# A hybrid decoder layer in one core: the second set's first product moved ahead in the first queries and keys, and one weight split moved between two additions of the output projection

## The chip, the cores and the metric

The kernel runs on one core of a Trainium2 chip. The metric is the device time of one execution in microseconds (us); lower is better. Runs of one kernel are summed up by their median.

## The reference

One decoder layer on x of 512 tokens by 1024 channels, all in float32, cut here to what the change touches:

```python
u = rmsnorm(x, ln1_g[i])
proj = u @ w_in[i]
q, k, v, pool_in, z, xbc, dt_raw, gate_pre = jnp.split(proj, split_idx, axis=-1)
y_a = dilated_attention_mixer(q, k, v, rel_bias) @ w_a[i]
y_b = pool_mixer(pool_in, pool_w[i], pool_scale[i]) @ w_b[i]
y_c = ssd_mixer(z, xbc, dt_raw, ...) @ w_c[i]
merged = gates[:, :, 0] * y_a + gates[:, :, 1] * y_b + gates[:, :, 2] * y_c
x = x + merged @ w_o[i]
x = x + conv_ffn(rmsnorm(x, ln2_g[i]), ...)
```

The attention has three groups of six heads of 64. The first group's queries and keys, 384 columns each, are three blocks of 128 columns of w_in for q and three for k. The output projection is `merged @ w_o`, 512x1024 by 1024x1024.

## The kernel before

**Jobs.** The work is a list of jobs, written by the generator `program`. A job is one piece of a weight matrix and the products that use it. Each float32 weight is split in two: a high part `wh`, rounded by a cast on ScalarE (`cast`, L200), and a low part `wl`, weight minus high part, by VectorE (`low`, L220). The activations are split in the same way. A product is then three groups of matmuls (`mm3`, L239), in the order wh by the high activation, wh by the low activation, wl by the high activation. So the low part of a weight is needed only for the last third of a product's matmuls. There are three buffers for high parts, two for low parts, and two for raw weights.

**Preparing ahead.** The loop at the end runs the jobs in order. Ahead of the body of job n it calls `prepare`, which issues the low part of job n+1, the cast of job n+2, and the load of job n+3. A job's `form` gives its weight where that isn't loaded but lies in a tile that sums are made in, and its `then` is run right behind its low part. A job that is marked `at_once` has the cast that it prepares issued whole at that place; otherwise the cast comes in two halves, between the matmuls of its body (`second`, `flush`). With `low_apart` the low part of the next job is not issued by `prepare` but kept as `low_next`, for the body to call. Each of TensorE, ScalarE, VectorE and GpSimd works off its instructions in the order in which the program issues them (`manual_schedule`); SyncE issues the loads.

**Sets of seven.** A product of two by two blocks is done in seven products in place of eight, "one" to "seven", with sums of weight quarters and of activations (`sevens`, `set_of_sevens`). `W[0]` and `W[1]` are quarters in memory. "one" uses W[0] as loaded; its `then`, `first_sum`, adds W[1] to W[0] on VectorE (L354) and issues two DMAs on GpSimd's queue that add another quarter into W[1] in memory (L375). "five" uses W[0] after that sum. "two" and "three" have raw quarters of their own, and "seven" uses W[1] after the two accumulating DMAs.

The queries and keys of the first group are two sets: set 0, with two blocks of q and two of k (256 columns a job, 24 matmuls of 128x256), and set 1, the half set, with the third block of each (128 columns, 12 matmuls). Both start from weights loaded far ahead: two loads (L750) and four (L745). Four banks of PSUM (`ROLE`) serve set 0 and set 1's "one", "six", "seven" and "four". They are taken from the rotation that the job before, the second of `v_jobs`, uses for its four accumulators `pb`; they come free when ScalarE has copied them out, each in two copies, v (L586) and dtr (L588). The first job of set 0 takes the first of them.

The second v job is `at_once`. `prepare` ahead of it issues the low part of set 0's "one" with the sum behind it, and the cast of the job after that; then come its matmuls, the copies of its banks, and a step of other work: one block of the pooling branch, as a difference pd on VectorE (L976), its cast pdh on ScalarE (L978), and its low part pdl on VectorE (L979). GpSimd makes the running sums psw for it (L967, L968). sal and sbl (L338, L339) are low parts of the activation sums that "five" and others use.

**Output projection.** `wo_sevens` does `merged @ w_o` in seven jobs in the order one, two, five, three, six, seven, four, each of 24 matmuls of 128x512 in two halves (i = 0, 1). After each half `use` adds the bank into the residual (L1369). "five" opens the banks Z; "three" goes on adding into the same banks. A bank that is being read by an addition can't be added to by a later product until the addition is done. `norm_early` (L446) starts the next norm on GpSimd.

Of the kernel before, what the change touches and what calls it, by code (L numbers as in the profile page):

```python
# [83 lines left out]
def trunk(ctx: ExitStack, tc, out, x, rel_bias, ln1_g, w_in, b_gate, w_a, pool_w, pool_scale, w_b,  # L84
# [23 lines left out]
    def T(name, dt=F32, shape=(P, S)):  # L108
        return big.tile(list(shape), dt, name=name, tag="t")
# [321 lines left out]
    def norm_turn(us, uh, ul, tb):  # L431
        for h in range(2):
            ps = SM("uT")
            for j in range(4):
                pe.transpose(ps[:, j * P:(j + 1) * P], us[h][:, j * P:(j + 1) * P], eye)
            pv = ps.rearrange("p (j t) -> p j t", j=4)
            hh = uh[:, 4 * h:4 * h + 4, tb * P:(tb + 1) * P]
            act.copy(hh, pv)  # L438
            dve.tensor_sub(ul[:, 4 * h:4 * h + 4, tb * P:(tb + 1) * P], pv, hh.bitcast(F32))

    def norm_early(t, g, h=0, mean=True):

        ss, v0 = (cpool.tile([P, 1], F32, name=f"{n}_{len(V0)}") for n in ("s0", "v0"))
        xg = T("xg")
        squares(act, t, ss)
        pool.tensor_tensor(xg, t, g[:, h * S:h * S + S], OP.mult)  # L446
        V0.append((v0, ss))
        if mean:
            mean_of(v0, ss)
        return v0, xg  # L450
# [4 lines left out]
    def norm_late(t, g, v0, outs, both=False, h=1):  # L455

        ss, v, sq, r, rt = (small(n, [P, 1]) for n in ("ss", "v", "sq", "r", "rt"))
        squares(act, t, ss)
        xg = T("xg")
        dve.tensor_tensor(xg, t, g[:, h * S:h * S + S], OP.mult)  # L460
        dve.scalar_tensor_tensor(v, ss, 1.0 / D, v0, OP.mult, OP.add)
        act.activation(sq, v, AF.Sqrt)
        yield xg
        dve.reciprocal(r, sq)
        dve.scalar_tensor_tensor(rt, r, v, r, OP.mult, OP.mult)
        dve.tensor_scalar(rt, rt, -0.5, 1.5, OP.mult, OP.add)
        if both:
            dve.tensor_tensor(r, r, rt, OP.mult)
            (o, a), (p, b) = outs(xg)
            dve.tensor_scalar(o, a, r, None, OP.mult)  # L470
            act.mul(p, b, r)
            return
        for o, src in outs(xg):
            dve.tensor_scalar(o, src, r, rt, OP.mult, OP.mult)
# [873 lines left out]
    def wo_sevens():  # L1348

        q = lambda two, h: w_o[:, h * S:h * S + S].rearrange("(k two p) c -> two p k c", two=2, p=P)[two]  # L1350
        W, X, Y, Z, r, means = {}, {}, {}, {}, {}, []

        def load():
            both_ = upool.tile([P, KD, S], F32R, name="ws", tag="uh").bitcast(F32)
            W["five"], W["six"] = both_[:, :4, :], both_[:, 4:, :]
            sp.dma_start(W["five"], q(0, 0))
            sp.dma_start(W["six"], q(1, 1))

        def add():
            for name, src in (("seven", q(0, 1)), ("four", q(1, 0))):  # L1360
                W[name] = ypool.tile([P, 4, S], F32, name="w3", tag="xs")
                sp.dma_start(W[name], src)
            for name, src in (("five", q(0, 1)), ("seven", q(1, 1)), ("six", W["five"]),
                              ("four", W["six"])):
                for k in (0, 2):
                    pool.dma_start(W[name][:, k:k + 2, :], src[:, k:k + 2, :], accum_op=OP.add)

        def plus(tb, h, what, op=OP.add):
            dve.tensor_tensor(X1[tb, h], X1[tb, h], what, op)  # L1369

        def late_norm(tb, h):
            if "uh" not in nxt:
                nxt["uh"] = upool.tile([P, KD, S], F32R, name="uh2", tag="uh")
                nxt["ul"] = upool.tile([P, KD, S], F32R, name="ul2", tag="ul")
            v0, xg0 = nxt[tb]
            us = [T("u0"), T("u1")]
            it = norm_late(X1[tb, h], nxt["g2"], v0, lambda xg1: ((us[1 - h], xg0), (us[h], xg1)),
                           True, h)
            next(it)

            def rest():
                next(it, None)
                yield
                norm_turn(us, nxt["uh"], nxt["ul"], tb)
            return rest()

        def use(name, i):
            if name == "one":
                plus(i, 0, X[i])
                if i:  # L1390
                    next(pair_sums[3])
                    next(pair_sums[3])
            elif name == "two":
                plus(i, 0, Y[i])
                nxt[i] = norm_early(X1[i, 0], nxt["g2"], mean=False)
                means.append(V0[-1])
            elif name == "five":
                plus(2 + i, 1, Z[i])
            elif name == "three":
                plus(i, 1, Z[i])  # L1400
                if i:
                    for _ in range(2):
                        mean_of(*means.pop(0))
            elif name == "six":
                plus(i, 1, X[i], OP.subtract)
                r[i] = late_norm(i, 1)
                if i:
                    next(r[0])
                    next(r[1])
            elif name == "seven":  # L1410
                plus(2 + i, 1, X[i], OP.subtract)
                nxt[2 + i] = norm_early(X1[2 + i, 1], nxt["g2"], 1, mean=False)
                means.append(V0[-1])
                if i:
                    next(r[0], None)
                    next(r[1], None)
                else:
                    jobs[name].low_next()
            else:
                if i:  # L1420
                    late_split.pop(0)()
                plus(2 + i, 0, X[i])
                mean_of(*means.pop(0))
                r[i] = late_norm(2 + i, 0)
                late.append(r[i])
                if i == 0:
                    next(r[i])

        banks = {"one": X, "six": X, "seven": X, "four": X, "five": Z, "three": Z, "two": Y}
        jobs = {}  # L1430

        def make(name, source=None):
            def body(ws):
                wh, wl = ws
                parts = [MS[SIDES[name], p] for p in range(4)]
                fresh = name in ("one", "two", "five")
                if name == "two":
                    for _ in pair_sums[3]:
                        pass
                if name == "four":  # L1440
                    late_split.append(jobs[name].prepare(later=True))
                if name == "one":
                    for i in range(2):
                        Y[i] = MM("p2")
                    for i in range(2):
                        X[i] = MM("p1")
                if name == "five":
                    for i in range(2):
                        Z[i] = SM("p5")
                for i in range(2):  # L1450
                    o = slice(i * P, (i + 1) * P)
                    mm3(banks[name][i], lambda k: wh[:, k, :], lambda k: wl[:, k, :],
                        lambda k: parts[k][0][:, o], lambda k: parts[k][1][:, o], range(4),
                        fresh, True, flip=True, again=not fresh)
                    use(name, i)
                    if i:
                        step()
            job = jobs[name] = Job([source] if source is not None else [], 4, S, body)
            if source is None:
                job.load = lambda: None  # L1460
                job.form = lambda: W[name]
            job.late = name == "four"
            job.at_once = True
            job.low_apart = name == "seven"
            return job

        return load, add, [make("one", q(0, 0)), make("two", q(1, 0)), make("five"),
                           make("three", q(1, 1)), make("six"), make("seven"), make("four")]


# [236 lines left out]
    def program():  # L1707
# [9 lines left out]
        for i, job in enumerate(v_jobs(0)):  # L1717
            job.at_once = True
            yield job
            if i == 0:  # L1720
                yield Call(lambda: ahead(sets0[0][1][n] for n in ("two", "three")))
        for i, name in ((0, "one"), (0, "five"), (1, "one"), (0, "two"), (1, "five"), (0, "three"),
                        (1, "two"), (1, "three"), (0, "six"), (1, "six"), (0, "seven"), (1, "seven"),
                        (0, "four"), (1, "four")):
            yield sets0[i][1][name]
# [77 lines left out]
    jobs = list(program())  # L1803
# [219 lines left out]
```

## Time and profile before

| | us |
|---|---|
| median of 3 runs | 1032.05 |
| lowest, highest run | 1031.59, 1032.14 |
| profiled execution, its time | 1030.83 |
| its span, first to last instruction | 1029.1 |
| TensorE busy | 1015.2 |
| VectorE busy | 738.8 |
| ScalarE busy | 502.7 |
| GpSimd busy | 181.3 |

The mean granted clock of TensorE is 0.996. Times inside the profile count from the span's start. Rows of the order of time give the start, the duration, the engine, the line of the kernel, the operation, output and inputs with their sizes, how many instructions are merged, and in brackets the idle time ahead of it on that engine and what ended it. PE is TensorE, DVE is VectorE, ACT is ScalarE, POOL is GpSimd, SP is SyncE, PEld is TensorE's load of the stationary operand. A matmul's duration reaches over the start of the next one, so merged rows overlap a little.

### The profile page before, as it was taken

How to read it: one execution, taken by the hardware profiler on the slowest of the kernel's cores; microseconds unless marked ns; L12 is line 12 of the kernel's file. 1: busy time of each engine (PE TensorE's matmuls, PEld its weight loads, DVE VectorE, ACT ScalarE, POOL GpSimd, SP SyncE). 2: the span in 40 equal slices, each digit the busy share in tenths (PEclk: the TensorE clock that was granted, in tenths of full speed). 3: DMA queues.
4: the chain of work that ended last, by engine and by line, in shares of the span. 5: the costliest groups of instructions: out<-in, count | busy, mean ns of one | idle time of the engine just before them, and what ended most of it. 6: DMA issues, size and time to landing. Idle time of an engine off the chain costs nothing.

```text
span 1029.1 us, 14051 instructions
## 1 busy us (share of the span) xinstructions
PE 1015.2 (99%) x5504; PEld 867.5 (84%) x5504; DVE 738.8 (72%) x1022; ACT 502.7 (49%) x859; POOL 181.3 (18%) x147
## 2 busy tenths in 40 slices
PE   9998999999999999999999999999999999999997
PEld 9988878899998888888888888898888888888885
DVE  6786775777767758767668768866768677666775
ACT  6434655445536664566455235654444443443342
POOL 1592000001100004310144611201111001111120
PEclk9998999999999999999999999999999999999999
DMA  9326521137543335552243779333233224323142
GB/s 295 107 67 127 190 83 45 62 63 193 130 111 123 89 98 148 135 135 59 82 150 128 268 145 285 123 122 105 82 118 118 91 82 164 123 83 122 61 144 82
DMA packets 122129, 127.11 MB, mean 124 GB/s; under 512 B 5811, under 2 KB 103414, under 8 KB 122063
## 3 DMA queue, kind: packets, MB, share of 16 engines
q1 hardware_dynamic: 115999, 118.02, 36.4%
q0 software_dynamic: 5472, 7.34, 4.7%
q8 instruction: 43, 0.70, 0.3%
q10 hardware_dynamic: 592, 0.86, 0.2%
q14 instruction: 23, 0.19, 0.1%
HBM read 120.31 MB, written 2.22 MB: 119 GB/s over the span
## 4 chain that ended last, share of the span: by engine, by line
PE 92%; POOL 3%; DVE 2%; issue 1%; ACT 1%; DMA 0%; SPq 0%; POOLq 0%; DVEq 0%; ACTq 0%
PE pa L239 30%; PE p L239 22%; PE pu L239 22%; PE pqk L239 3%; PE pb L239 2%; PE pa L1870 2%; POOL psw L967 2%; PE ps L850 1%; PE pu L1638 1%; PE pt L878 1%; PE ppw L239 1%; PE po L891 1%; PE py L1176 1%; POOL psw L968 1%; PE pa L1827 1%
## 5 line engine op out<-in xcount | busy, mean ns | idle before, releaser
L220 DVE TENSOR_TENSOR wl<-raw,wh 128x2048 fp32r<-128x2048 f32 (+3 forms) x88 | 192.6, 2190 | 36.2 <-ACT wh L200 23.3
L200 ACT CAST wh<-raw 128x1024 fp32r<-128x1024 f32 (+3 forms) x174 | 166.9, 980 | 47.7 <-DVE raw L344 25.5
L1499 DVE SCALAR_TENSOR_TENSOR hc<-pu,fcol,hc 128x510 f32<-128x510 f32 x88 | 65.9, 748 | 59.9 <-ACT hc L1496 58.2
L239 PE MATMUL pa<-uh,wh 128*128 128x512 f32 x336 | 86.5, 399 | 0.0
L239 PE MATMUL pu<-uh,wl 128*128 128x512 f32 (+1 forms) x352 | 83.7, 380 | 0.0
L239 PE MATMUL pu<-uh,wh 128*128 128x512 f32 (+1 forms) x352 | 83.6, 380 | 0.0
L239 PE MATMUL pu<-ul,wh 128*128 128x512 f32 (+1 forms) x352 | 83.5, 379 | 0.0
L239 PE MATMUL pa<-ul,wh 128*128 128x512 f32 x336 | 83.0, 389 | 0.0
L239 PE MATMUL pa<-uh,wl 128*128 128x512 f32 x336 | 83.0, 389 | 0.0
L1504 POOL TENSOR_TENSOR hc<-hc 128x512 f32<-128x512 f32 x22 | 30.4, 1380 | 274.8 <-DVE hc L1499 225.9
L239 PEld LDWEIGHTS pu<-uh,wl 128*128 128x128 f32 x352 | 64.1, 188 | 12.8 <-DVE wl L220 0.3
L239 PEld LDWEIGHTS pu<-uh,wh 128*128 128x128 f32 x352 | 64.1, 188 | 12.6 <-ACT uh L438 0.2
L239 PEld LDWEIGHTS pu<-ul,wh 128*128 128x128 f32 x352 | 64.2, 188 | 12.5
L239 PEld LDWEIGHTS pa<-ul,wh 128*128 128x128 f32 x336 | 63.1, 188 | 13.3
L239 PEld LDWEIGHTS pa<-uh,wl 128*128 128x128 f32 x336 | 63.1, 188 | 13.1
L239 PEld LDWEIGHTS pa<-uh,wh 128*128 128x128 f32 x336 | 61.2, 188 | 12.8 <-issue 0.7
L1496 ACT ACTIVATE hc<-pu,fcol,fcol 128x512 f32<-128x512 f32 x40 | 31.2, 780 | 81.3 <-PE pu L239 81.0
L200 ACT CAST wh<-w 128x512 fp32r<-128x512 f32 (+3 forms) x78 | 50.1, 686 | 28.8 <-DVE w L354 17.2
L220 DVE TENSOR_TENSOR wl<-w,wh 128x1024 fp32r<-128x1024 f32 (+3 forms) x39 | 54.0, 1385 | 10.6 <-ACT wh L200 5.8
L375 POOL DMA_DIRECT2D w<-in_w_in_dram x14 | 17.2, 1231 | 194.1 <-DVE w L354 140.2
L871 ACT ACTIVATE sb<-sb,both 128x128 f32<-128x128 f32 (+1 forms) x72 | 30.1, 418 | 31.8 <-DVE both L868 21.7
L1501 ACT ACTIVATE hc<-hc 128x512 f32<-128x512 f32 x22 | 13.9, 632 | 42.9 <-DVE hc L1499 42.9
(400 smaller groups left out, 2033.9 us busy)
## 6 DMA issues: line engine op xcount, KB each, us to landing
raw<-in_ffn_w_up_dram SPq DMA_DIRECT2D x22, 1024.0 KB, 5.1
raw<-in_w_in_dram SPq DMA_DIRECT2D x21, 1024.0 KB, 5.3
raw<-in_ffn_w_down_dram SPq DMA_DIRECT2D x11, 1024.0 KB, 4.8
raw<-in_w_in_dram SPq DMA_DIRECT2D x16, 512.0 KB, 4.9
raw<-in_w_b_dram SPq DMA_DIRECT2D x4, 1024.0 KB, 4.7
al<-ad SPq DMA_DIRECT2D x16, 256.0 KB
raw<-in_w_c_dram SPq DMA_DIRECT2D x4, 1024.0 KB, 5.3
w<-in_ffn_w_down_dram SPq DMA_DIRECT2D x4, 1024.0 KB
```

Source lines behind the costliest of these rows:

```text
L200: act.copy(job.high[:, :, o], job.raw[:, :, o])
L220: (eng or dve).tensor_tensor(l[:, :, o], job.raw[:, :, o], h[:, :, o].bitcast(F32), OP.subtract)
L239: pe.matmul(ps, l, r, start=first and n == 0, stop=last and n == total - 1, skip_group_check=again)
L375: pool.dma_start(W[1][:, k:k + 2, at:at + n], src[:, k:k + 2, :], accum_op=OP.add)
L850: pe.matmul(pss[i][:, o:o + w * P], q[r, n * P:(n + 1) * P], k[r, kb * P:(kb + w) * P], start=True, stop=True)
L871: act.activation(sb[:, off:off + w * P], sb[:, off:off + w * P], AF.Exp, bias=nm[:, n, h:h + 1], accum_out=ls[:, n, h:h + 1])
L967: pool.tensor_tensor(nxt[:, sh:], cur[:, sh:], cur[:, :S - sh], OP.add)
L1496: act.activation(t, ps, AF.Identity, bias=ff["c1"][:, ff["b"] + m:ff["b"] + m + 1], scale=fw(2, m))
L1499: dve.scalar_tensor_tensor(t[:, sh:], ps[:, :S - sh], fw(k, m), t[:, sh:], OP.mult, OP.add)
L1501: act.activation(t, t, AF.Silu)
L1504: pool.tensor_tensor(a, a, t, OP.mult)
L1870: pe.matmul(first[2 * n + j][:, lo:hi], a[:, k, j * P:(j + 1) * P], b[:, k, lo:hi], start=a is wh and b is uh and k == 0, stop=a is wl and ...
```

## The change

Two edits that have no instruction in common. In the order of the first sets, set 1's "one" comes second, ahead of set 0's "five" and not behind it. In the output projection the third job, "five", is marked `low_apart`, and the low part of the fourth job, "three", is issued by `use` after the first of the two additions of "five", where it was issued ahead of the matmuls of "five". No instruction is added or taken away.

```diff
             elif name == "five":
                 plus(2 + i, 1, Z[i])
+                if i == 0:
+                    jobs[name].low_next()
...
             job.at_once = True
-            job.low_apart = name == "seven"
+            job.low_apart = name in ("five", "seven")
...
-        for i, name in ((0, "one"), (0, "five"), (1, "one"), (0, "two"), (1, "five"), (0, "three"),
+        for i, name in ((0, "one"), (1, "one"), (0, "five"), (0, "two"), (1, "five"), (0, "three"),
                         (1, "two"), (1, "three"), (0, "six"), (1, "six"), (0, "seven"), (1, "seven"),
                         (0, "four"), (1, "four")):
             yield sets0[i][1][name]
```

## The prediction

> **What bounds the kernel now.** I read the page first (busy time of each engine), then the list of who waited for whom on TensorE, then the busy and clock table of four short stretches, then the order of time of every engine around the two places that the change touches.
>
> ```profile
> PE 1015.2 (99%) x5504; PEld 867.5 (84%) x5504; DVE 738.8 (72%) x1022; ACT 502.7 (49%) x859; POOL 181.3 (18%) x147
> ```
> ```profile
> PE p L239 <- ACT dtr L588: 4.7, 1, 4.7
> ```
> ```profile
> 77.80:81.20 3.40, 0.53 (x3) 1.00 0.85 246
> 81.20:84.60 3.40, 1.53 (x7) 0.50 1.00 221
> 84.60:88.00 3.40, 3.40 (x18) 0.50 0.45 73
> 88.00:91.40 3.40, 3.40 (x30) 0.99 0.63 77
> ```
>
> TensorE is the bound: it is busy 1015.2 us of a span of 1029.1, so only 13.9 us are idle, and one wait holds 4.7 of them. What does not shorten a wait of TensorE or raise its clock is worth nothing. In the table of stretches (start:end, length, PE busy, count, granted clock, DMA share, GB/s) the reader sees a second price of that wait: the clock falls to 0.50 after the stretch in which TensorE was busy 0.53 of 3.4 us, and stays there for 6.8 us.
>
> **Place one, the first sets of seven products.** All engines in order of time:
>
> ```profile
> 77.45 0.89 PE L239 MATMUL pb<-wl,uh 128*128 128x400 f32 x4
> 83.06 1.22 PE L239 MATMUL p<-uh,wh 128*128 128x256 f32 x4 [4.73 <-ACT dtr L588]
> 88.23 0.64 PE L239 MATMUL p<-sah,wh 128*128 128x256 f32 x4
> 91.10 0.64 PE L239 MATMUL p<-uh,wh 128*128 128x256 f32 x4
> 92.54 0.64 PE L239 MATMUL p<-uh,wh 128*128 128x256 f32 x4
> 73.42 0.62 ACT L978 CAST pdh<-pd 128x512 fp32r<-128x512 f32 x1 [3.39 <-DVE pd L976]
> 81.42 1.14 ACT L200 CAST wh<-w 128x512 fp32r<-128x512 f32 x2 [7.39 <-DVE w L354]
> 82.84 0.17 ACT L588 COPY dtr<-pb 128x16 f32<-128x16 f32 x1
> 84.73 0.78 ACT L200 CAST wh<-w 128x256 fp32r<-128x256 f32 x2
> 77.63 0.69 DVE L338 TENSOR_TENSOR sal<-sa,sah 128x512 fp32r<-128x512 f32 x1 [1.74 <-POOL psw L968]
> 78.87 1.21 DVE L220 TENSOR_TENSOR wl<-w,wh 128x1024 fp32r<-128x1024 f32 x1
> 80.11 1.22 DVE L354 TENSOR_TENSOR w<-w 128x1024 f32<-128x1024 f32 x1
> 81.25 0.68 DVE L976 SCALAR_TENSOR_TENSOR pd<-psw,pu 128x512 f32<-128x512 f32 x1
> 84.93 0.69 DVE L979 TENSOR_TENSOR pdl<-pd,pdh 128x512 fp32r<-128x512 f32 x1 [2.99 <-ACT pdh L978]
> 85.53 1.22 DVE L220 TENSOR_TENSOR wl<-w,wh 128x1024 fp32r<-128x1024 f32 x1
> 88.50 0.69 DVE L220 TENSOR_TENSOR wl<-w,wh 128x512 fp32r<-128x512 f32 x1 [1.74 <-PE p L239]
> 89.22 0.69 DVE L354 TENSOR_TENSOR w<-w 128x512 f32<-128x512 f32 x1
> ```
>
> Read as a chain: the second v job ends at 78.3. The full set's "one" (83.06) needs the first of the v job's four banks, and that is freed by ScalarE's copy dtr at 83.01. ScalarE stood 7.39 us in front of the cast at 81.42, which is that of "five". It waits for the sum w (80.11 to 81.33), which stands behind the low part of "one" (78.87), and that behind sal (77.63), which waits for GpSimd. The v copies are queued behind that cast. The four products in order are "one" 83.06, "five" 88.23, half set's "one" 91.10, "two" 92.54. "one" takes 5.17 us, "five" with as many matmuls 2.87: the half clock costs 2.30.
>
> **The reordering, step by step.** Nothing is added or removed; all that is issued for a job (its low part, sum, casts, accumulating DMAs) moves with it.
>
> (1) Before the second v job ScalarE now casts the half set's "one" (0.78, row 84.73) and not "five". Its weight quarters need no sum. They are long there:
>
> ```profile
> 19.96 1.88 SPq L745 DMA_DIRECT2D w<-in_w_in_dram  x1
> ```
>
> That is the last of the half set's four loads. So the cast runs right behind pdh (74.04), ends near 74.9, and the v copies follow each bank. TensorE has its bank and continues at 78.2. The wait of 4.73 and the half clock go: 7.03 us at most.
>
> (2) What is late next is VectorE. The low part of "one" is unmoved, ending at 80.08. A 128x256 matmul goes every 0.12 us (four per 0.48, rows 91.10 to 92.54 are twelve in 1.44). The first eight of "one" need no low part: 78.2 to 79.15, then a wait to 80.15, 1.0 us. The other sixteen end at 82.07.
>
> (3) The half set's "one": its low part comes on VectorE behind the sum (to 81.33), pd (81.25), a pass through ScalarE and pdl. With ScalarE free pdl starts 1.37 after pd, as in this pair:
>
> ```profile
> 72.70 0.68 DVE L976 SCALAR_TENSOR_TENSOR pd<-psw,pu 128x512 f32<-128x512 f32 x1
> 74.07 0.76 DVE L979 TENSOR_TENSOR pdl<-pd,pdh 128x512 fp32r<-128x512 f32 x1 [0.69 <-ACT pdh L978]
> ```
>
> So pdl at 82.62, the low part (0.69) 83.23 to 83.92. Eight matmuls end at 83.03: a second wait of 0.95, end of the job 84.47. Its sum is moved too (0.69, to 84.65), and its accumulating DMAs, behind (6).
>
> (4) "five": both cast halves (1.14) follow pdh on ScalarE at 82.6 and end near 83.7. Its low part (1.22) follows the half set's sum, to 85.8. Eight matmuls end at 85.43: a third wait, 0.42, end at 87.8. "two" then has its casts (85.6) and low part (87.0) in time. The buffers of the low parts (two) are free: the one for "five" at 82.1, for "two" at 84.5.
>
> (5) "two" starts at 87.8 where it started at 92.54: 4.75 less. Three restarts cost some 0.1 each (the group after the wait at 645.71 below takes 1.17 where the one at 647.64 takes 1.08). I take 4.5. The bounds: no new wait at all, 7.0; all three waits double, 7.0 less 4.7, 2.3.
>
> (6) The queues moved past. GpSimd's accumulations:
>
> ```profile
> 81.67 1.38 POOL L375 DMA_DIRECT2D w<-in_w_in_dram  x1 [3.27 <-DVE w L354]
> 87.18 1.24 POOL L375 DMA_DIRECT2D w<-in_w_in_dram  x1 [4.13 <-issue]
> 92.06 1.20 POOL L375 DMA_DIRECT2D w<-in_w_in_dram  x1 [3.65 <-issue]
> 95.88 1.24 POOL L375 DMA_DIRECT2D w<-in_w_in_dram  x1 [2.61 <-issue]
> DMA to landing us min/median/max: 3.5/4.6/5.4
> 110.02 0.64 PE L239 MATMUL p<-sbh,wh 128*128 128x256 f32 x4
> ```
>
> They follow each other at 3.8 to 5.5 us, about one landing time, and not their sums, so the half set's two stay at 92.06 and 95.88 and the last lands by 99.4 to 101.3. The half set's "seven" (110.02) uses it and would start at 105.5; its two casts take 0.8 (row 84.73), so 3 us are to spare. SP's loads follow the raw buffers that VectorE frees and move with TensorE. I cost this at nothing; with the cover gone each us that the landing comes after 104.7 is a us lost.
>
> **Place two, the output projection.**
>
> ```profile
> 642.68 1.07 PE L239 MATMUL p<-wh,sah 128*128 128x512 f32 x4
> 644.50 1.07 PE L239 MATMUL p<-wl,sah 128*128 128x512 f32 x4
> 645.71 1.17 PE L239 MATMUL p<-wh,sbh 128*128 128x512 f32 x4
> 647.64 1.08 PE L239 MATMUL p<-wl,sbh 128*128 128x512 f32 x4
> 642.01 2.95 DVE L220 TENSOR_TENSOR wl<-raw,wh 128x2048 fp32r<-128x2048 f32 x1
> 644.89 1.40 DVE L1369 TENSOR_TENSOR x<-x,p 128x512 f32<-128x512 f32 x2
> 646.21 2.29 DVE L220 TENSOR_TENSOR wl<-ws,wh 128x2048 fp32r<-128x2048 f32 x1
> 641.53 4.59 POOL L446 TENSOR_TENSOR xg<-x,grow 128x512 f32<-128x512 f32 x2 [12.10 <-DVE x L1369]
> ```
>
> Groups of four start 0.91 apart (642.68, then 644.50 two groups on). The fourth job, "three" (645.71), should start at 645.41. It adds into the bank that the first addition of "five" reads, and that addition stood behind the low part of "three" (642.01 to 644.96), to 645.58. With the restart, three groups take 3.14 from 644.50 where 2.72 is normal: 0.4 us lost. The change puts the addition first: the half product is done at 642.85, the addition takes 0.7, the low part runs 643.55 to 646.5 at its slow 2.95, the second addition to 647.2. "three" needs the low part in its third group, at 645.41 + 1.81 = 647.2: 0.7 to spare. Behind the waiting addition VectorE has only this low part; the low part of "six" (646.21) comes near 647.2 and ends at 649.5, for a group at 652.7. SP's next load of up weights is freed 1.5 us later and lands ahead of three more jobs. Gain 0.4; bounds: 0.4 gained and, by the low part waiting out GpSimd's second product (to 646.12) and then 2.29, at 648.4, a loss of 1.2, net -0.8.
>
> **The sum.** -4.5 - 0.4 = -4.9. The profiled execution took 1030.83 (span 1029.1), 1.22 below the median of the runs, so it would come to 1025.9, and the median 1032.05 to 1027.1.
>
> [...] The row: the clock fell after a stretch busy 16% and came back only after one busy in full; the new stretches at the same times would be busy about 70% (77.8 to 79.15 and 80.15 to 81.2 are 2.4 of 3.4), and no row here shows what the clock does then. [...]
>
> The row at 642.01: a low part started 0.48 us into GpSimd's product and took 2.95 where alone it takes 2.29. [...]
>
> **The rivals.** (a) The clock halves again at the short waits. From 81.2 to 88.0 the matmuls take 0.213 (24 in 5.17 with the tail): "one" ends at 82.8, the half "one" at 85.3, "five" at 89.3, since the waits fill up. 1.5 less gain: 1028.6. If it holds one stretch more, 1.7 more: 1030.3. For it: three waits in 8 us. Against: 70% is far from 16%. Chance 0.12.
> (b) The low part of "three" is fully blocked by GpSimd: 1028.3. Against: 2.95. Chance 0.08.
> (c) The reordering does not do what it says: ScalarE is held ahead of the v copies all the same, by the half set's weights or a buffer of the high part. Only place two stays: 1031.6. Against: the load at 19.96. Chance 0.07.
> (d) Slower: GpSimd's accumulations into the half set's W[1]. If they land late, "seven" waits. A landing after 104.7 begins to cost; to pass the old time by 0.2% it must eat 4.9 + 2.1 = 7.0 more, a landing near 111.7, 16 us after the issue at 95.88. Against: 3.5 to 5.4. Chance 0.04.
> (e) The new waits are half as long or less: 1025.9 down to 1024.6. Chance 0.03.
>
> **How the numbers follow.** The forecast has 0.66: 1027.1. What a measurement can tell from no change is 0.2%, 2.06 us. Faster: forecast, (b), (e) and most of (a): 0.66 + 0.08 + 0.03 + 0.10 = 0.87. Same: (c) and the rest of (a): 0.09. Slower: (d), 0.04. The range is 1025.2 to 1029.6: from between the two ends of (e) to between the two ends of (a), leaving out (c), (d) and some of (a), about 0.15.
>
> **What would show it.** TensorE goes on at 78.2 with no wait on dtr; its largest waits in 78 to 88 are three of 0.4 to 1.0 us on wl; granted clock 1.00 there; "two" begins near 88; the v copies come before the cast of "five". At 641 "three" follows "five" without a gap. Wrong would be a clock of 0.50 after 81, a wait on ScalarE before the first product, or an idle time before the half set's "seven".

## The result and the profile after

The changed kernel takes 1025.64 us (median of 4 runs, 1025.19 to 1025.91), the kernel before 1031.82 beside it (4 runs, 1030.14 to 1032.14). The ratio is 0.9943, 95% interval 0.9926 to 0.996: faster by 6.2 us by the medians. The profiled execution took 1025.91 with a span of 1024.1, against 1030.83 and 1029.1: 4.9 and 5.0 less.

TensorE's longest waits in the profile after:

```profile
PE p L239 <- DVE wl L220: 1.7, 3, 0.8
PE pa L1829 <- DVE relb L512: 1.1, 1, 1.1
```

The 4.7 us on dtr are gone; in their place stand three waits on low parts, 1.7 us in all. The same stretches as before (length, PE busy, granted clock, DMA share, GB/s):

```profile
77.80:81.20 3.40, 2.57 (x19) 1.00 0.71 217
81.20:84.60 3.40, 2.68 (x23) 1.00 1.01 243
84.60:88.00 3.40, 3.22 (x26) 1.00 0.55 80
88.00:91.40 3.40, 3.40 (x31) 1.00 0.56 73
```

TensorE is busy 76% and 79% of the two stretches in which it was busy 16% and 45%, and the clock stays at 1.00. In order of time, TensorE, then ScalarE, then VectorE:

```profile
77.85 0.90 PE L239 MATMUL pb<-wl,uh 128*128 128x400 f32 x4
78.59 0.63 PE L239 MATMUL p<-uh,wh 128*128 128x256 f32 x4
79.06 0.64 PE L239 MATMUL p<-ul,wh 128*128 128x256 f32 x4
80.53 0.73 PE L239 MATMUL p<-uh,wl 128*128 128x256 f32 x4 [0.83 <-DVE wl L220]
81.10 0.64 PE L239 MATMUL p<-uh,wh 128*128 128x256 f32 x4
84.37 0.74 PE L239 MATMUL p<-uh,wl 128*128 128x256 f32 x4 [0.72 <-DVE wl L220]
86.23 0.74 PE L239 MATMUL p<-sah,wl 128*128 128x256 f32 x4 [0.18 <-DVE wl L220]
88.25 0.64 PE L239 MATMUL p<-uh,wh 128*128 128x256 f32 x4
74.33 0.71 ACT L200 CAST wh<-w 128x256 fp32r<-128x256 f32 x2
75.31 0.17 ACT L588 COPY dtr<-pb 128x16 f32<-128x16 f32 x1
82.89 1.14 ACT L200 CAST wh<-w 128x512 fp32r<-128x512 f32 x2
79.26 1.21 DVE L220 TENSOR_TENSOR wl<-w,wh 128x1024 fp32r<-128x1024 f32 x1
83.02 0.69 DVE L979 TENSOR_TENSOR pdl<-pd,pdh 128x512 fp32r<-128x512 f32 x1 [0.69 <-ACT pdh L978]
83.63 0.68 DVE L220 TENSOR_TENSOR wl<-w,wh 128x512 fp32r<-128x512 f32 x1
84.96 1.22 DVE L220 TENSOR_TENSOR wl<-w,wh 128x1024 fp32r<-128x1024 f32 x1
```

ScalarE now has the half set's cast (74.33) ahead of the copies, the first bank is free at 75.5, and the first product goes on without a wait at 78.59. The cast of "five" comes at 82.89. This execution reached the v job 0.40 later, so I compare from the v job's last group to the start of "two": 15.09 before (77.45 to 92.54), 10.40 now (77.85 to 88.25), 4.69 less. The output projection:

```profile
638.41 1.07 PE L239 MATMUL p<-wh,sah 128*128 128x512 f32 x4
641.13 1.07 PE L239 MATMUL p<-wh,sbh 128*128 128x512 f32 x4
642.95 1.07 PE L239 MATMUL p<-wl,sbh 128*128 128x512 f32 x4
638.62 0.69 DVE L1369 TENSOR_TENSOR x<-x,p 128x512 f32<-128x512 f32 x1 [0.84 <-PE p L239]
639.22 2.75 DVE L220 TENSOR_TENSOR wl<-raw,wh 128x2048 fp32r<-128x2048 f32 x1
637.26 2.55 POOL L446 TENSOR_TENSOR xg<-x,grow 128x512 f32<-128x512 f32 x2 [12.32 <-DVE x L1369]
```

From the second half of "five" (638.41) to the third group of "three" (642.95) it is 4.54 where it was 4.96 (642.68 to 647.64): 0.42 less and no gap. The two edits give 5.11 and the later start took 0.40 back, which leaves 4.71 of the 5.0 by which the spans differ; where the other 0.3 comes from stays open.

### The profile page after: what moved, and what is told of

Its sections match the earlier page's. It is cut to its first block, busy times and chain, and to the rows that moved or that the text cites. A ratio compares the mean times of both kernels' runs of the same rounds, so it can differ in the third digit from the quotient of the medians.

```text
span 1024.1 us, 14050 instructions
## 1 busy us (share of the span) xinstructions
PE 1013.5 (99%) x5504; PEld 865.9 (85%) x5504; DVE 738.2 (72%) x1022; ACT 502.6 (49%) x859; POOL 178.9 (17%) x147
## 4 chain that ended last, share of the span: by engine, by line
PE 93%; POOL 3%; DVE 2%; ACT 1%; issue 1%; POOLq 0%; DVEq 0%; ACTq 0%
PE pa L239 30%; PE p L239 23%; PE pu L239 22%; PE pqk L239 3%; PE pb L239 2%; PE pa L1872 2%; POOL psw L967 2%; PE ps L850 1%; PE pu L1640 1%; PE pt L878 1%; PE ppw L239 1%; PE po L891 1%; PE py L1176 1%; POOL psw L968 1%; PE pa L1829 1%
## 5 line engine op out<-in xcount | busy, mean ns | idle before, releaser
L239 PE MATMUL pa<-uh,wh 128*128 128x512 f32 x336 | 86.5, 399 | 0.0
```

The source lines that it names most:

```text
L239: pe.matmul(ps, l, r, start=first and n == 0, stop=last and n == total - 1, skip_group_check=again)
```

## The experiments

Differences are against the kernel before or the changed kernel as named. The theory: ScalarE stood ahead of the v copies with a cast that waited for a sum, the idle time that followed halved the clock, and the low parts on VectorE bound the stretch after it.

**Each edit alone.** `order_alone` has only the new order:

```diff
-        for i, name in ((0, "one"), (0, "five"), (1, "one"), (0, "two"), ...
+        for i, name in ((0, "one"), (1, "one"), (0, "five"), (0, "two"), ...
```

> The reordering without the edit of the output projection. Theory (ScalarE stood with the v copies behind a cast that waited for a sum, and the half clock followed from the idle time): the second product set goes on right behind the v job, three waits of 0.8, 0.7 and 0.2 us on low parts are left, granted clock 1.00; 4.7 us less than before, by the profile of before some 1026.1 us. In the output projection the 0.3 us gap ahead of the fourth job stays, so it is 0.4 us slower than the changed kernel. Rival (the two edits help each other, or the output projection carries a good part): more than 1 us slower than the changed kernel.

```profile
77.90 0.90 PE L239 MATMUL pb<-wl,uh 128*128 128x400 f32 x4
88.30 0.64 PE L239 MATMUL p<-uh,wh 128*128 128x256 f32 x4
640.19 1.07 PE L239 MATMUL p<-wl,sah 128*128 128x512 f32 x4
643.33 1.08 PE L239 MATMUL p<-wl,sbh 128*128 128x512 f32 x4
```

It took 1026.53 (5 runs, 1026.10 to 1027.15); ratio to before 0.9966, interval 0.9954 to 0.9979. The same three waits are left, 1.7 us, clock 1.00, and from the v job's last group to "two" it is 10.40 again. The time fell by 3.8 us between the medians where 4.7 was expected; the kernel before beside it ran at 1030.35 (27 runs). The varying price of the half clock, measured below, is part of that.

By the medians it is 0.9 us slower than the changed kernel in the first comparison and 1.1 slower than in the later `after_again`, where 0.4 was expected and the rival had more than 1. These groups did not run side by side, so the times alone do not refute the rival. The profiles speak for the theory: the spans differ by 0.4, the reordered place takes the same 10.40, and in the output projection three groups still take 3.14 (640.19 to 643.33), where the changed kernel takes 2.72 (640.23 to 642.95).

`low_alone` has only `low_next` and `low_apart` for "five" in the output projection.

> The edit of the output projection without the reordering. Theory: 0.4 us less than before, that is no difference that can be measured in the time; in the profile the fourth job follows the third without a gap, and the 4.73 us wait on dtr and the clock of 0.50 are as before. Rival (the low part is held by GpSimd's product): a new wait on wl of about 1 us in the fourth job.

It took 1029.64 (11 runs), ratio 0.9994, interval 0.9985 to 1.0003: no difference that the time can show, as expected. In its profile "three" follows "five" at 0.91 like any group, with no wait on wl. So the rival of a low part held for a whole microsecond falls.

**The clock's price by itself.** `filler` is the kernel before with work that nothing reads in the idle time:

```diff
+        def keep_busy():
+            ps = SM("busy")
+            for _ in range(20):
+                pe.matmul(ps[:, :P], ones, ones, start=True, stop=True)
+        yield Call(keep_busy)
         for i, name in ((0, "one"), (0, "five"), (1, "one"), (0, "two"), ...
```

> The kernel before, with 20 matmuls of ones into an unused bank put between the second v job and the first product, work that nothing reads. They keep TensorE busy while it waits for the v copies. Theory (the wait costs 4.7 us as idle time and 2.3 us more as half clock): the first product still starts near 83.1, but takes 2.9 us and not 5.2, granted clock 1.00; 2.3 us less than before. Rival (the half clock does not come from the idle time, or the slow first product has another cause): first product at 5.2 us, time as before or longer.

```profile
77.74 0.89 PE L239 MATMUL pb<-wl,uh 128*128 128x400 f32 x4
78.47 4.62 PE L1725 MATMUL busy<-ones 128*128 128x128 f32 x40
83.35 0.74 PE L239 MATMUL p<-uh,wh 128*128 128x256 f32 x4 [0.26 <-ACT dtr L588]
86.32 0.64 PE L239 MATMUL p<-sah,wh 128*128 128x256 f32 x4
```

The row counts 40 records for the 20 matmuls of ones. The first product starts 5.61 after the v job's last group began, exactly as before, but takes 2.97 and not 5.17. It took 1028.62 (11 runs), 1.7 less between the medians; ratio 0.9986, interval 0.9977 to 0.9995. So the half clock is the idle time's second price, and of the expected 2.3 some 1.7 came. What the difference is, a second profile of the kernel before shows.

> The kernel before, for a second profile of it. [...]

TensorE in the kernel before, second profile (1030.27 us, span 1028.5):

```profile
77.98 0.89 PE L239 MATMUL pb<-wl,uh 128*128 128x400 f32 x4
83.58 1.23 PE L239 MATMUL p<-uh,wh 128*128 128x256 f32 x4 [4.71 <-ACT dtr L588]
87.82 0.64 PE L239 MATMUL p<-sah,wh 128*128 128x256 f32 x4
92.14 0.64 PE L239 MATMUL p<-uh,wh 128*128 128x256 f32 x4
```

The idle time is the same, but the first product takes 4.24 and not 5.17. `low_alone`, which has the same idle time, gives a third: 83.05 to 87.95, 4.90. Cut into stretches of 1 us, the clock was 0.50 from 81.2 to 88.0 in the first profile (6.8 us), from 80.6 to 87.5 in `low_alone` (6.8), and from 83.1 to 86.5 here (3.4). So the half clock lasted 6.8, 6.8 and 3.4 us, and cost 2.3, 2.0 and 1.4 us (5.17, 4.90 and 4.24 less the 2.87 that as many matmuls took at the full clock). This is part of why the kernel before scatters over 1029.5 to 1032.5 in all its runs here, and the changed kernel, without it, over 1025.2 to 1026.1. Of the 51 later runs of the kernel before, each with its mean granted clock, the 13 at 0.997 have a median of 1029.79 us and the 6 at 0.994 one of 1031.31. The clock is not the whole of that scatter: the slowest run, 1032.54, has 0.995.

**ScalarE's place, with the old order.** `cast_later`:

```diff
         for i, job in enumerate(v_jobs(0)):
-            job.at_once = True
+            job.at_once = i == 0
```

> The order of before, but the second v job is no longer at_once: the cast of set 0's five comes in two halves, the first behind the v copies of two of the four banks, the second behind the others. Theory (what counted was ScalarE's waiting cast ahead of the copies): the first product starts right behind the v job; five then waits near 1 us for its bank, since two copies are still behind the first half of the cast, and near 2 us for its low part; two starts near 89.5 where it was 92.5; 3.0 us less than before, 1.7 more than with the reordering. Rival A (the order of the products as such brings the gain): no gain, within 0.5 us of before. Rival B (any way to free the first bank brings all): 4.7 less.

```profile
78.48 0.63 PE L239 MATMUL p<-uh,wh 128*128 128x256 f32 x4
82.42 0.64 PE L239 MATMUL p<-sah,wh 128*128 128x256 f32 x4
86.13 0.74 PE L239 MATMUL p<-sah,wl 128*128 128x256 f32 x4 [2.59 <-DVE wl L220]
89.59 0.64 PE L239 MATMUL p<-uh,wh 128*128 128x256 f32 x4
84.60:88.00 3.40, 1.87 (x15) 1.00 0.44 68
```

It took 1027.70 (11 runs), 2.65 less than before between the medians (3.0 expected), ratio 0.9976, interval 0.9967 to 0.9985. The first product goes on at once, "five" waits 2.59 for its low part, "two" starts at 89.59 (89.5 expected). The wait for a bank did not come; the one for the low part was 2.59 where some 2 were expected. Both rivals fall: the order is not needed to lose the 4.7 us wait, and freeing the bank alone does not bring all of it. What the new order adds is that a short product without a sum covers the long chain ahead of "five". The last row is worth a look: TensorE is idle for 2.59 in one piece, and the clock stayed at 1.00. That holds for the profiled execution, with a mean clock of 0.999. Seven of the 11 runs have 0.999 and take 1027.02 to 1027.89; the other four have 0.996 to 0.998 and take 1028.52 to 1029.36. So in some executions the same wait seems to cost the half clock as well, but none of those was profiled.

**How much room the moved low part has.** `low_after_both` calls `low_next` after the second addition (`if i == 1`).

> The changed kernel, but in the output projection the low part of the fourth job comes behind the second of the two additions. Theory (the low part has 0.7 us to spare between the additions, and costs what it comes too late): it starts near 641.9 on the changed kernel's clock and ends at 644.2, for a third group due at 642.95; a new wait on wl of 1.2 us, 1.3 us more than the changed kernel. Rival (the place of this low part does not count as long as it is off the front): no wait, same time as the changed kernel.

```profile
643.68 1.21 PE L239 MATMUL p<-wl,sbh 128*128 128x512 f32 x4 [1.17 <-DVE wl L220]
```

It took 1026.80 (5 runs) against 1025.46 for the changed kernel beside it (`after_again`, 1025.30 to 1026.13): 1.34 more, and one new wait of 1.17. Both are as expected, and the rival falls.

> The changed kernel as it is, once more, as the measure for the three beside it. Theory: its profile has no half clock and the same three waits on low parts (0.83, 0.72, 0.18 us), so its runs scatter less than those of the kernel before, whose half-clock stretch can begin and end at different places. Rival (the scatter comes from elsewhere): both scatter alike.

Its three waits are 0.83, 0.70 and 0.16, its clock 1.00, and its ratio to before is 0.9948 (0.9936 to 0.9961).

**The waits that are left.** `pd_later` moves one pooling block a step back, `(2, 2, 2, 2, 3, 3, 6, 7)[m]` where the seventh number was 5.

> The changed kernel with one block of the pooling branch (pd, pdh, pdl of block 6) one step later, that is behind the half set's one and not ahead of its low part. Theory (the second and third wait stand behind the pass pd, pdh, pdl on VectorE): the low part of the half set's one comes 2.0 us earlier, both waits (0.72 and 0.18) and their restarts (0.1 each) go, 1.1 us less than the changed kernel; the first wait of 0.83 stays. Rival (VectorE is full anyway, the waits move on): two waits elsewhere in the set, no gain.

It took 1026.01 (5 runs, 1025.52 to 1026.74), no gain. The second and third wait are gone: from the v job's last group (78.26) to "two" (87.26) it is 9.00, 1.4 less than the changed kernel. But a new wait gives that back. First the rows of `pd_later` (SP, GpSimd, ScalarE, TensorE), then those of the changed kernel (`after_again`):

```profile
92.82 0.37 SPq L188 DMA_DIRECT2D raw<-in_pool_w_dram  x1
92.41 1.20 POOL L375 DMA_DIRECT2D w<-in_w_in_dram  x1 [3.55 <-DVE wl L220]
100.55 1.24 POOL L375 DMA_DIRECT2D w<-in_w_in_dram  x1 [6.94 <-DMA raw<-in_pool_w_dram]
105.39 0.41 ACT L200 CAST wh<-w 128x256 fp32r<-128x256 f32 x1 [4.12 <-DMA w<-in_w_in_dram]
106.42 0.74 PE L239 MATMUL p<-sbh,wh 128*128 128x256 f32 x4 [1.53 <-ACT wh L200]
```

```profile
93.40 0.37 SPq L188 DMA_DIRECT2D raw<-in_pool_w_dram  x1
91.84 1.20 POOL L375 DMA_DIRECT2D w<-in_w_in_dram  x1 [3.64 <-issue]
95.80 1.24 POOL L375 DMA_DIRECT2D w<-in_w_in_dram  x1 [2.75 <-issue]
```

With the set 1.4 us earlier, the 1 MB load of the pooling weights comes 0.4 us behind GpSimd's third accumulating DMA and not 1.6. The third then took 7.8 us from issue to landing, to 100.2, where it took 3.6 in the changed kernel. The fourth was issued at 100.55 and not at 95.80, and the half set's "seven" waited for it. The bracket names the load as what the fourth waited for, but the load took 5.0 us and had landed by 97.8. In both profiles each of these DMAs is issued 0.3 us behind the landing of the one before, so it was the third that held the fourth. That the load close behind it slowed the third is argued from the order of the two, and not shown. This is the forecast's rival (d) at work, in a kernel one step on. The profiled execution, 1026.74, is the slowest of the five, so the others may have lost less there.

`both_later` also takes the activation sums a step back (`enumerate((0, 0, 5, 7))` for 6).

> As pd_later, and the last pair of activation sums also one step later, so that its low part sal, which waits 1.75 us for a buffer that GpSimd holds, stands behind the low part of set 0's one and not ahead of it. Theory (the first wait comes from that buffer): the low part of one is ready near 77.9, no wait on low parts is left between 78 and 90; 1.7 of waits and 0.3 of restarts, 2.0 us less than the changed kernel. Rival (the buffer's wait moves to the sum or the cast behind it): five waits for its cast or its low part near 1 us, gain of 1.1 or less beside pd_later.

```profile
79.30 0.62 ACT L336 CAST sbh<-sb 128x512 fp32r<-128x512 f32 x1 [3.55 <-POOL psw L968]
81.56 0.48 ACT L586 COPY v<-pb 128x384 f32<-128x384 f32 x1 [1.03 <-POOL psw L968]
82.16 1.23 PE L239 MATMUL p<-uh,wh 128*128 128x256 f32 x4 [3.68 <-ACT dtr L588]
```

It took 1029.03 (11 runs), 3.6 slower than the changed kernel. Neither the theory nor the rival had this: the low part of "one" came at 76.0 as wanted, but the wait for GpSimd's buffer moved to ScalarE, to the cast sbh and the v copy itself, ahead of the copies. The old wait was back at 3.68, with the half clock behind it. It fails for the very reason that the change works.

`pd_local` is `pd_later` with the half set's accumulating DMAs replaced by one addition on GpSimd, from a quarter that is loaded already:

```diff
+            def sums():
+                dve.tensor_tensor(W[0], W[0], W[1], OP.add)
+                pool.tensor_tensor(W[1], W[1], W[3], OP.add)
+            jobs["one"].then = sums
         return load, jobs
```

> As pd_later, and the half set's two accumulating DMAs on GpSimd's queue are replaced by one addition on GpSimd, from the quarter that lies in memory already. Theory (the reordering's queue risk: in pd_later the half set's seven waited 1.5 us because the last accumulating DMA was issued at 100.55, behind the load of the pooling weights, and not at 95.9): that wait goes, the two waits that pd_later took away stay away, only the wait of 0.83 on the first low part is left; 1.1 to 1.4 us less than the changed kernel. Rival (the moved pooling block costs time elsewhere): a new wait of 1 us or more on ScalarE or VectorE, no gain.

```profile
PE p L239 <- DVE wl L220: 0.8, 1, 0.8
88.03 1.79 POOL L828 TENSOR_TENSOR w<-w 128x512 f32<-128x512 f32 x1
```

It took 1024.64 (5 runs, 1024.46 to 1024.88); the changed kernel beside it 1025.66 (`after_third`, 1025.41 to 1025.91).

> The changed kernel again, as the measure beside pd_local on the same chip. No theory expects another time than before: near 1025.5 us.

So it is 1.0 less than the changed kernel (1.1 to 1.4 expected), with no overlap of the runs, and 0.9944 of before (0.9932 to 0.9957). Only the first wait is left. It is the fastest version of this study.

## Why the prediction was right, and where it was off

**The chain was right.** ScalarE's waiting cast ahead of the v copies held the first bank: taking it away by the order or by the cast's place (`cast_later`) ends the 4.7 us wait, and putting another wait in ScalarE's way (`both_later`) brings it back.

**The three new waits.** Counted from group start to group start with their restarts, they cost 1.08, 0.97 and 0.43 (79.06 to 81.10, two groups on, is 2.04 where 0.96 is normal, and so on), 2.48 in all; the forecast had 2.37 for the waits and 0.3 for the restarts. The gain of the reordering was 4.69 where 4.5 was taken, and "two" came at 88.25 on a clock 0.40 later, where 87.8 was worked out.

**The output projection.** 0.42 where 0.4 was forecast. The low part was ready at 641.97 for a group at 642.95, 1.0 us to spare and not 0.7. Being 1.2 us late costs 1.3, as `low_after_both` shows.

**The sum.** 4.9 was forecast against the profiled execution, and its times differ by 4.9. That it fits to a tenth is partly luck: with the second profile of the kernel before, which takes 14.16 from the v job's last group to "two" (77.98 to 92.14), the reordering would have gained 3.76 and not 4.69. The medians differ by 6.2, so the median came 1.5 below the 1027.1. The step that was off is the last one: carrying the sum over to a median that lay 1.2 above the profiled execution. That profile paid the most half clock of three, and still lay below three of the four runs of its group. Beside the later runs the kernel before had medians of 1030.35, 1030.78 and 1030.57, and the changed kernel was 5.3 and 4.9 below it. Why the four runs of the first comparison lay a microsecond higher stays open.

**A term sized from one execution.** The half clock was taken at a fixed 2.30. In three profiles it was 2.3, 2.0 and 1.4, and `filler` brought 1.7. A range would have been right here.

**The rivals.** (a) did not come: 76% and 79% busy kept the full clock, and three waits of 0.8, 0.7 and 0.2 us did not lower it: the clock is 1.00 from 77.8 to 91.4 in all three profiles of the changed kernel. (c) did not come. (d) did not decide this change, but "3 us to spare" was the wrong kind of number: it took the accumulating DMAs as fixed in time, and in `pd_later`, where a load had moved with TensorE, the last one went out 4.7 us later.

**A row misread.** For (b) I took GpSimd's two products at 2.3 us each, half of 4.59. Taken one by one in the profile before, the first (641.53) took 1.29 us and the second (642.79) 3.33; in the profile after they took 1.29 and 1.28. A low part with no product beside it took 2.28 (642.49 in the profile after) and 2.29 (646.21 before); the one that came 0.48 us into the first product before took 2.95 (642.01), and the one that came 0.69 us into the second product after (638.53) took 2.75 (639.22). So in these rows the low part took 0.5 to 0.7 us more beside a product; which of the two held the other is not shown. With the pair at 2.57 the second product would have ended at 644.1, and a low part begun only then, at 2.29, at 646.4, ahead of the 647.2 at which it was needed. That is an estimate from these rows, and by it (b) was overpriced.

## What to carry to other kernels

When the bound engine waits for a buffer, look at what stands ahead of the releasing copy in its engine's queue; a cast that waits for a sum there costs the whole sum's chain, and a short piece of work without that dependency, put between, hides it. Count a long idle time of TensorE twice, once as it is and once as the half clock that can follow, and give the second a range: 1.4 to 2.3 us behind the 4.7 here, and nothing in the profile with 2.59. Before moving work ahead, check the transfers that do not move with it against those that do.

## What the runs showed of the hardware

Four profiles show the half clock. It came 2.9 us after TensorE fell idle in the first profile of the kernel before, 4.2 in `before_look`, 3.2 in `both_later` and 2.3 in `low_alone`, and lasted 6.8, 3.4, 3.4 and 6.8 us. TensorE's busy share of the 3.4 us ahead of it, of its first 3.4 us, and of three stretches at the full clock in profiles without it:

| profile | stretch | busy | clock behind it |
|---|---|---|---|
| `before_look` | 79.66 to 83.06, full clock | 0% | half |
| `both_later` | 78.31 to 81.72, full clock | 5% | half |
| before, first profile | 77.82 to 81.22, full clock | 15% | half |
| `low_alone` | 77.24 to 80.64, full clock | 32% | half |
| `cast_later` | 82.75 to 86.15, full clock | 24% | full |
| `cast_later` | 84.60 to 88.00, full clock | 55% | full |
| after | 77.80 to 81.20, full clock | 76% | full |
| `low_alone` | 80.64 to 84.06, half clock | 30% | half |
| before, first profile | 81.22 to 84.63, half clock | 46% | half |
| `before_look` | 83.06 to 86.46, half clock | 85% | full |
| `both_later` | 81.72 to 85.14, half clock | 87% | full |

The stretch of `cast_later` that holds its wait of 2.59 us is busy 24%, less than the 32% of `low_alone`, and the clock stayed full. So the busy share alone does not tell these cases apart, and what does is not shown.
